# The value columns of the input projection as one token-major product of 512 columns

## The chip, the cores and the metric

The kernel runs on one core of one Trainium2 chip. The metric is the device time of one execution in microseconds (us), lower is better; a kernel's time is the median of its runs. Engines are named as in the profile: PE is TensorE (its matrix products) and PEld its weight loads, DVE is VectorE, ACT is ScalarE, POOL is GpSimd, SP is the queue that issues most transfers from memory (DMA).

## The reference

One layer of a decoder over 1024 tokens of width 1024, all in float32. The part that the change touches is the first projection:

```
h = rms_norm(x, mix_pre_norm)
z = h @ w_in                                   # 1024 x 2816
q_a, k_a, v_a, q_h, f_h, i_h, g_h = split(z)   # 512, 128, 128, 512, 512, 512, 512 columns
attn = sliding_window_sink_attention(q_a, k_a, v_a, sinks)   # the banded part
rec  = hgrn2_group(q_h, f_h, i_h, g_h, ...)    # 4 heads; i_h holds the heads' values
x = x + rms_norm(concat(attn, rec) @ w_out)
```

After it come a cross-attention into 256 memory tokens (4 heads; each head's values times its rows of `ca_wo` is one 256 x 1024 matrix, `VW`), and a gated MLP with a convolution of width 3.

## The kernel before

**Precision.** A float32 product is made of three products of reduced-precision parts: every operand is split into a high part (a cast on ACT) and a rest (a subtraction, on DVE or POOL), and high x high, high x low and low x high are summed in PSUM. `split` (lines 72 to 74) is that pair of instructions; its rows in the profile all carry L73 and L74.

**Layouts.** A product either puts features on partitions (`feat`, `feat_part`: the weight stands, 512 or 256 tokens stream through) or tokens on partitions (`wide_block`: a block of 128 tokens stands, the weight's columns stream). `wide_block` is used where the next step wants tokens on partitions: for the banded attention's values `va` and for the values `vh` of the recurrence's heads 0 to 2 (head 3 goes through `feat` and is transposed). The width 1024 of the contraction is 8 steps `k`, so a block of 128 tokens takes 8 x 3 = 24 products.

**The first token pass** (the loop `for q in range(4)`, lines 275 to 294). Each turn takes two blocks of 128 tokens: their normalised rows are transposed on PE (`turn_block`, L127, 16 transposes), split into `hTh`, `hTl` (L129 on ACT, L132 on DVE), multiplied with the K columns (`feat_part`, L227, 24 products of 256 columns into `pk`), and with a 256-column piece of `w_in` (`wide_block`, L256): 128 columns of `va` and the 128 of head 0. Two turns share one PSUM tile `pv` of four blocks, which ACT then copies out with two instructions of 512 columns (L293, L294). Meanwhile the next two blocks of x are normalised (L89 on ACT, L83 and L84 on POOL, L114 on DVE).

**The four head groups** (`for j in range(4)`, lines 591 to 636). Each makes the banded query `pqa`, and for the recurrence `pg`, `pq`, `pf`, with `feat` (48 products of 512 columns each). At j = 1 a second `wide_block` stage makes heads 1 and 2: 8 blocks, again 256 columns, copied out on L608. Between products, `tick()` lets the two lanes, the banded attention (`swa`) and the recurrence (`hgrn`), issue one step of their work: once every 6 products of 512 columns in `feat`, once every 12 of 256 columns in `wide_block`.

**Weights.** The table `order` lists all weight pieces of these stages in their order of use; `load_next` (lines 161 to 181) issues the loads, and `ahead` (lines 183 to 195) keeps loads and splits a few pieces ahead. Which engine makes the rest of a split is chosen by one expression that uses the piece's index `n` in `order`:

```
t = split_u(t, "w", (P, KD, P) if kind == "cols" else (P, 1024),
            pool if n == 0 or arg[0][0] is a["ca_wo"] and n % 2 else dve)
```

So of the eight pieces of `ca_wo`, two for each head of `VW` (L813), those at odd places of `order` are split on POOL, the others on DVE.

**PSUM.** The pool `pj` holds two tiles of 1024 columns, the pool `sm` four of 512 columns, each taken in turn. Within an engine instructions run in the order that a scheduler gave them when the program was built; `order` rows below show that order.

## Time and profile before

| | before |
|---|---|
| median of three runs | 1417.96 us (1416.31 to 1418.66) |
| the profiled execution | 1420.67 us |
| its span, first to last instruction | 1418.5 us |
| mean granted clock of TensorE | 0.993 |
| PE busy | 1385.2 us, 98% of the span |
| DVE, ACT, POOL busy | 893.1, 649.7, 164.7 us |

A row of the timeline gives the start of an instruction in us from the span's start, how long it took, its engine, line and operation, what it writes and reads with sizes, how many equal ones were merged, and in brackets how long its engine had been idle before it and what ended that. A product's own duration runs over its successor's start, since products are pipelined; what a product occupies PE for is read from start to start.

### The profile page before, as it was taken

What the parts mean: (1) busy time and instruction counts of PE and PEld (TensorE: products, weight loads), DVE (VectorE), ACT (ScalarE), POOL (GpSimd) and SP (SyncE); (2) the same over time, 40 slices, a digit from 0 to 9 for tenths busy, and PEclk for the clock granted to TensorE, in tenths of its full rate; (3) what the DMA queues carried; (4) which work ended last, traced back from release to release, by engine and by line L of the source; (5) the groups of instructions that cost most, each with busy time, mean ns of one, the idle gap of its engine ahead of it and who ended that gap; (6) DMA issues with size and microseconds to landing.
All of it is one profiled execution on the core that took longest, in us unless ns stands there. A gap on an engine that the chain in (4) does not pass through costs nothing.

```text
span 1418.5 us, 21778 instructions
## 1 busy us (share of the span) xinstructions
PE 1385.2 (98%) x8638; PEld 1157.0 (82%) x8638; DVE 893.1 (63%) x1273; ACT 649.7 (46%) x1185; POOL 164.7 (12%) x258
## 2 busy tenths in 40 slices
PE   7999999999999999999999899999999999999997
PEld 6988887877898888887888788888888888788886
DVE  4456617565674553458336998888888887645572
ACT  4463523635464333345334554554554555444440
POOL 3100100101010110002111121111111130000020
PEclk9999999999999999999999999999999999999999
DMA  7231102111843252014222376666655676977651
GB/s 232 53 82 46 46 8 54 31 47 60 209 135 119 90 163 60 7 40 149 89 89 90 86 189 171 177 171 178 170 162 160 168 208 236 328 242 223 223 194 60
DMA packets 157412, 186.04 MB, mean 131 GB/s; under 512 B 17221, under 2 KB 104702, under 8 KB 157310
## 3 DMA queue, kind: packets, MB, share of 16 engines
q1 hardware_dynamic: 145694, 155.81, 35.1%
q0 software_dynamic: 11616, 28.84, 8.6%
q8 instruction: 68, 1.11, 0.3%
q14 instruction: 34, 0.28, 0.1%
HBM read 136.12 MB, written 45.35 MB: 128 GB/s over the span
## 4 chain that ended last, share of the span: by engine, by line
PE 92%; DVE 3%; ACT 2%; DMA 1%; issue 1%; POOL 1%; SPq 1%; DVEq 0%; POOLq 0%; ACTq 0%
PE xz L939 23%; PE dn L1165 14%; PE co L680 6%; PE po L680 6%; PE cq L236 5%; PE y L939 4%; PE pqa L236 3%; PE pm L653 3%; PE pf L236 3%; PE pv L256 3%; PE pq L236 3%; PE pg L236 3%; PE cq L227 2%; PE sc L768 1%; PE po L448 1%; PE lv L463 1%
## 5 line engine op out<-in xcount | busy, mean ns | idle before, releaser
L939 PE MATMUL xz<-th,w 128*128 128x512 f32 x960 | 305.2, 392 | 0.0
L939 PEld LDWEIGHTS xz<-th,w 128*128 128x128 f32 x960 | 180.2, 188 | 44.5 <-DVE ug L1041 4.0
L939 PE MATMUL xz<-tl,w 128*128 128x512 f32 x480 | 187.2, 390 | 0.0
L74 DVE TENSOR_TENSOR dnl<-dn,dnh 128x1024 fp32r<-128x1024 f32 x77 | 90.5, 1219 | 56.0 <-ACT dnh L73 53.6
L1165 PE MATMUL dn<-dnl,dnh 128*128 128x512 f32 x308 | 121.3, 394 | 2.7 <-DVE dnl L74 2.7
L1165 PE MATMUL dn<-dnh,dnl 128*128 128x512 f32 x308 | 121.0, 393 | 0.0
L1165 PE MATMUL dn<-dnh 128*128 128x512 f32 x308 | 120.0, 392 | 0.0
L939 PEld LDWEIGHTS xz<-tl,w 128*128 128x128 f32 x480 | 90.2, 188 | 17.3
L73 ACT CAST dnh<-dn 128x1024 fp32r<-128x1024 f32 x77 | 76.8, 1053 | 48.9 <-PE dn L1165 21.1
L74 DVE TENSOR_TENSOR wl<-w,wh 128x1024 fp32r<-128x1024 f32 x59 | 73.1, 1250 | 29.8 <-ACT wh L73 29.7
L73 ACT CAST wh<-w 128x1024 fp32r<-128x1024 f32 x64 | 66.1, 1052 | 11.7 <-DMA w<-in_ca_wq 4.9
L1165 PEld LDWEIGHTS dn<-dnl,dnh 128*128 128x128 f32 x308 | 58.5, 190 | 15.8 <-DVE dnl L74 3.5
L1165 PEld LDWEIGHTS dn<-dnh,dnl 128*128 128x128 f32 x308 | 58.6, 190 | 12.2
L1165 PEld LDWEIGHTS dn<-dnh 128*128 128x128 f32 x308 | 58.5, 190 | 12.1
L953 DVE SCALAR_TENSOR_TENSOR c<-uv,par,c 128x1023 f32<-128x1023 f32 x22 | 28.2, 1284 | 63.8 <-ACT c L952 63.8
L74 DVE TENSOR_TENSOR w<-w,w 128x512 fp32r<-128x512 f32 x105 | 66.8, 683 | 0.4 <-ACT w L73 0.4
L73 ACT CAST w<-w 128x512 fp32r<-128x512 f32 x105 | 59.6, 618 | 0.0
L939 PE MATMUL y<-th,w 128*128 128x512 f32 x168 | 55.2, 389 | 0.0
L952 ACT ACTIVATE c<-ug,par 128x1024 f32<-128x1024 f32 x22 | 27.4, 1245 | 41.3 <-DVE ug L1041 41.1
L83 POOL TENSOR_SCALAR rstd<-ss 128x1 f32<-128x1 f32 x42 | 14.3, 341 | 230.6 <-ACT y L89 139.0
L680 PE MATMUL po<-wh,mh 128*128 128x512 f32 x128 | 40.0, 393 | 0.0
L680 PE MATMUL co<-VWh,pth 128*128 128x512 f32 x128 | 40.0, 393 | 0.0
(327 smaller groups left out, 3274.9 us busy)
## 6 DMA issues: line engine op xcount, KB each, us to landing
w<-in_ffn_w_up SPq DMA_DIRECT2D x44, 512.0 KB, 5.7
dn<-gd SPq DMA_DIRECT2D x77, 256.0 KB, 4.7
ws<-in_ffn_w_down POOLq DMA_DIRECT2D x66, 256.0 KB, 4.3
gd<-c SPq DMA_DIRECT2D x44, 256.0 KB, 2.3
wsd<-ws POOLq DMA_DIRECT2D x44, 256.0 KB, 2.7
dn<-wsd SPq DMA_DIRECT2D x44, 256.0 KB, 5.0
gd<-gt SPq DMA_DIRECT2D x33, 256.0 KB, 3.3
dn<-in_ffn_w_down SPq DMA_DIRECT2D x33, 256.0 KB, 4.3
```

The costliest lines, as they stand in the source:

```text
L73: act.copy(hi, src)
L74: eng.tensor_tensor(lo, src, hi.bitcast(F32), op=ALU.subtract)
L83: pool.tensor_scalar(r, ss, eps, None, op0=ALU.add)
L227: pe.matmul(ps[:, t0:t0 + n], l[:, k, :], r[:, k % 2, c:c + n], start=(m == 0), stop=(m == 23))
L236: pe.matmul(ps[:, half * 512:(half + 1) * 512], l[:, k, :], hts[half][k // 2][sel][:, k % 2, :], start=(k == 0 and j == 0), stop=(k == KD ...
L256: pe.matmul(ps[:, tb % 4, :], l[:, k % 2, c:c + P], r[:, k % 4, :], start=(m == 0), stop=(m == 23))
L653: pe.matmul(ps[:, i, :], l[:, k, :], r[:, k % 4, :], start=(n == 0), stop=(n == 23))
L680: pe.matmul(ps[:, ch * 512:(ch + 1) * 512], l, r[:, ch * 512:(ch + 1) * 512], start=(k == 0 and j == 0), stop=(k == KD - 1 and j == 2))
L939: pe.matmul(ps, l[k], r[k // 2][:, k % 2, :], start=start and m == 0, stop=stop and m == last, skip_group_check=True)
L952: act.activation(c, u, AF.Identity, scale=conv_w(2, j), bias=conv_b(j))
L953: dve.scalar_tensor_tensor(c[:, 1:], u[:, :T - 1], conv_w(1, j), c[:, 1:], op0=ALU.mult, op1=ALU.add)
L1165: pe.matmul(ps, l[:, 0, c], r[:, 1, :], start=start and k == 0, stop=stop and k == 2, skip_group_check=True)
```

## The change

The 256-column piece becomes one of 512 columns: `va` and heads 0, 1 and 2 together. It is loaded as four tiles of 256 rows of `w_in`, each by two transfers (128 columns and 384 columns), where there were two tiles of 512 rows. All of it is multiplied in the first token pass; the stage at j = 1, its weights and its 16 ticks are gone. A block's result is now one PSUM tile of the pool `sm` (it was a quarter of a `pj` tile), and each block is copied out at once, by four ACT copies of 128 columns.

```
-    order = [cols(w_in, (C_KA, P)), ("wide", [(w_in, C_VA, P), (w_in, C_IH, P)])]
+    order = [cols(w_in, (C_KA, P)), ("wide", [(w_in, C_VA, P), (w_in, C_IH, 3 * P)])]
     for j in range(4):
-        if j == 1:
-            order.append(("wide", [(w_in, C_IH + P, 2 * P)]))
...
-            t = [U("w", (P, 4, 256)) for _ in range(2)]
-            for i in range(2):
+            t = [U("w", (P, 2, 512)) for _ in range(4)]
+            for i in range(4):
                 o = 0
                 for w, c, n in arg:
-                    sp.dma_start(t[i][:, :, o:o + n], w[512 * i:512 * i + 512, c:c + n]
+                    sp.dma_start(t[i][:, :, o:o + n], w[256 * i:256 * i + 256, c:c + n]
                                  .rearrange("(k p) n -> p k n", p=P))
...
-                pe.matmul(ps[:, tb % 4, :], l[:, k % 2, c:c + P], r[:, k % 4, :],
+                pe.matmul(ps, l[:, k % 2, c:c + P], r[:, k % 2, :],
                           start=(m == 0), stop=(m == 23))
                 m += 1
-            if k % 4 == 3:
-                tick()
...
-        if q % 2 == 0:
-            ps_v = PJ("pv", (P, 4, 256))
         for tb in (2 * q, 2 * q + 1):
+            ps_v = SM("pv")
             wide_block(ps_v, first[1], hT, tb)
-        if q % 2 == 1:
-            act.copy(va[:, 2 * q - 2:2 * q + 2, :], ps_v[:, :, :P])
-            act.copy(vh0[:, 2 * q - 2:2 * q + 2, :], ps_v[:, :, P:])
+            for i, t in enumerate([va] + vh[:3]):
+                act.copy(t[:, tb, :], ps_v[:, i * P:(i + 1) * P])
...
-        if j == 1:
-            w = weight()
-            vh[1:3] = [U("vh", (P, NB, P)) for _ in range(2)]
-            for half in range(2):
-                ps = PJ("pv", (P, 4, 256))
-                for b in range(4):
-                    wide_block(ps, w, hT, half * 4 + b)
-                for i in range(2):
-                    act.copy(vh[1 + i][:, half * 4:half * 4 + 4, :], ps[:, :, i * P:(i + 1) * P])
```

Three places of the built order are spoken of below. The first is on PE, at the second turn of the first token pass, from its last transposes on (`tp`; `pk` is the K product, `pv` the value product). Before:

```order
L127 MATMUL tp_313<-ident,x_111 128x128 x4
L256 MATMUL pv_237<-wh_191,hTh_85 128x256
L227 MATMUL pk_127<-hTh_85,wh_147 128x256
L256 MATMUL pv_237<-wl_192,hTh_85 128x256
L256 MATMUL pv_237<-wh_191,hTl_86 128x256
```

and now:

```order
L127 MATMUL tp_338<-ident,x_111 128x128 x4
L225 MATMUL pk_133<-hTh_85,wh_155 128x256
L254 MATMUL pv_385<-wh_199,hTh_85 128x512
L254 MATMUL pv_385<-wl_200,hTh_85 128x512
L254 MATMUL pv_385<-wh_199,hTl_86 128x512
```

The value product, which needs one block's parts, stood ahead of the K product, which needs both blocks'; now the K product stands first.

The second is on ACT at the third turn: the copies out of `pv` and the casts of the transposed blocks. Before:

```order
L293 COPY va_128<-pv_237 128x512
L294 COPY vh_129<-pv_237 128x512
L129 CAST hTh_93<-tp_410 128x2x128
L129 CAST hTh_95<-tp_410 128x2x128
L129 CAST hTh_93<-tp_428 128x2x128
```

and now:

```order
L288 COPY va_134<-pv_414 128x128
L288 COPY vh_135<-pv_414 128x128
L288 COPY vh_136<-pv_414 128x128
L288 COPY vh_137<-pv_414 128x128
L129 CAST hTh_93<-tp_443 128x2x128
L129 CAST hTh_95<-tp_443 128x2x128
L129 CAST hTh_93<-tp_461 128x2x128
```

Two copies of 512 columns ahead of the casts at every second turn have become four of 128 columns at every turn (those of the block that ended last; the other block's stand earlier).

The third is on PE in the cross-attention, at the first head of `VW` (`vw`, made from the `ca_wo` pieces' parts `wh`, `wl`) and the first scores of the last head (`sc`). Before:

```order
L813 MATMUL vw_6394<-wl_6285,cvh_6274 128x512 [waits Pool_49]
L813 MATMUL vw_6448<-wh_6280,cvl_6275 128x512 x2
L768 MATMUL sc_6407<-ckh_6401,cqh_6268 128x256 [waits Activation_49]
L768 MATMUL sc_6464<-ckh_6401,cqh_6268 128x256
L813 MATMUL vw_6448<-wh_6284,cvh_6274 128x512 x2
L768 MATMUL sc_6407<-ckl_6402,cqh_6268 128x256 [waits DVE_49]
```

and now:

```order
L797 MATMUL vw_6232<-wl_6119,cvh_6112 128x512 [waits Pool_49]
L797 MATMUL vw_6286<-wh_6118,cvl_6113 128x512
L752 MATMUL sc_6245<-ckh_6239,cqh_6106 128x256 [waits Activation_49]
L797 MATMUL vw_6286<-wh_6118,cvl_6113 128x512
L752 MATMUL sc_6302<-ckh_6239,cqh_6106 128x256
L797 MATMUL vw_6286<-wh_6122,cvh_6112 128x512 x2
L797 MATMUL vw_6286<-wl_6123,cvh_6112 128x512 x2
L752 MATMUL sc_6245<-ckl_6240,cqh_6106 128x256 [waits DVE_49]
```

One list entry fewer moves every piece of `ca_wo` by one place, so the first piece of each pair is now split on POOL and the second on DVE, the other way round than before; and two products more stand ahead of the score that waits for DVE.

## Rows read from the trace of the kernel before

**Rows 1.** The profile's page: busy time, share of the span, number of instructions.

```profile
PE 1385.2 (98%) x8638; PEld 1157.0 (82%) x8638; DVE 893.1 (63%) x1273; ACT 649.7 (46%) x1185; POOL 164.7 (12%) x258
```

**Rows 2.** PE's longest waits, whole span: for whom, us in total, times, longest.

```profile
PE tp L127 <- DVE x L114: 9.3, 2, 7.9
PE dn L1165 <- DVE dnl L74: 2.7, 1, 2.7
```

**Rows 3.** Line 256: one of three equal forms; ns shortest/median/longest, first and last start.

```profile
L256 PE MATMUL pv<-wh,hTh x128: 277/283/386, 17.9 to 169.1; 128*128 128x256 f32 x128
```

**Rows 4.** Timeline of PE: 37 value products of 256 columns in a row.

```profile
31.20 0.28 PE L256 MATMUL pv<-wh,hTl 128*128 128x256 f32 x1
...
35.52 0.28 PE L256 MATMUL pv<-wh,hTl 128*128 128x256 f32 x1
```

**Rows 5.** Timeline of PE: 17 products of 512 columns in a row.

```profile
186.34 0.62 PE L236 MATMUL pq<-hTh,wh 128*128 128x512 f32 x2
...
189.97 0.39 PE L236 MATMUL pq<-hTh,wl 128*128 128x512 f32 x1
```

**Rows 6.** Timeline of PE: the later turns of the first token pass and its end.

```profile
23.64 1.91 PE L127 MATMUL tp<-ident,x 128*128 128x128 f32 x16
...
27.03 0.38 PE L256 MATMUL pv<-wh,hTl 128*128 128x256 f32 x1 [0.71 <-DVE hTl L132]
...
35.65 1.91 PE L127 MATMUL tp<-ident,x 128*128 128x128 f32 x16
37.31 0.36 PE L256 MATMUL pv<-wh,hTh 128*128 128x256 f32 x1
...
46.42 1.91 PE L127 MATMUL tp<-ident,x 128*128 128x128 f32 x16
...
57.19 0.25 PE L309 MATMUL pst<-ident,pv 97*128 97x97 f32 x1
```

**Rows 7.** Timeline of DVE at the second turn.

```profile
25.36 1.28 DVE L114 SCALAR_TENSOR_TENSOR x<-x,rstd,wmix 128x1024 f32<-128x1024 f32 x1 [0.77 <-POOL rstd L84]
```

**Rows 8.** ACT: timeline at the third turn; then a group (busy us, mean ns).

```profile
35.84 0.59 ACT L293 COPY va<-pv 128x512 f32<-128x512 f32 x1 [9.26 <-PE pv L256]
...
36.80 2.33 ACT L129 CAST hTh<-tp 128x256 fp32r<-128x256 f32 x8
...
L73 ACT CAST mh<-mTa 128x128 fp32r<-128x128 f32 x32 | 7.5, 297 | 1.1 <-PE po L680 1.1
```

**Rows 9.** Timeline of the first 20 us: the value piece's halves and the first value product.

```profile
14.32 1.05 ACT L73 CAST wh<-w 128x1024 fp32r<-128x1024 f32 x1 [0.40 <-DMA w<-in_w_in]
...
16.10 1.04 ACT L73 CAST wh<-w 128x1024 fp32r<-128x1024 f32 x1 [0.73 <-DMA w<-in_w_in]
...
17.18 1.23 DVE L74 TENSOR_TENSOR wl<-w,wh 128x1024 fp32r<-128x1024 f32 x1 [0.55 <-ACT wh L73]
...
17.89 0.28 PE L256 MATMUL pv<-wh,hTh 128*128 128x256 f32 x1
```

**Rows 10.** Timeline of POOL, DVE and PE in the cross-attention, one engine after another.

```profile
638.57 2.67 POOL L74 TENSOR_TENSOR wl<-w,wh 128x1024 fp32r<-128x1024 f32 x1 [9.18 <-ACT wh L73]
...
654.75 2.39 POOL L74 TENSOR_TENSOR wl<-w,wh 128x1024 fp32r<-128x1024 f32 x1 [8.79 <-ACT wh L73]
...
639.04 2.74 DVE L74 TENSOR_TENSOR ckl<-ckT,ckh 128x512 fp32r<-128x512 f32 x1
...
655.25 1.91 DVE L773 TENSOR_SCALAR cmx<-cmx 128x2 f32<-128x2 f32 x1
...
641.83 0.39 PE L768 MATMUL sc<-ckl,cqh 128*128 128x256 f32 x1 [1.45 <-DVE ckl L74]
...
659.03 0.70 PE L813 MATMUL vw<-wh,cvh 128*128 128x512 f32 x2 [2.02 <-DVE cri L780]
```

**Rows 11.** Busy time by stage: PE, PEld, DVE, ACT, POOL, then granted clock, DMA share, GB/s.

```profile
800.00:805.00 5.00, 4.72 (x11) 3.80 (x12) 4.35 (x7) 2.47 (x4) 0.00 (x0) 0.50 0.70 225
...
1220.00:1225.00 5.00, 5.00 (x13) 3.90 (x12) 4.58 (x5) 3.26 (x4) 0.00 (x0) 0.50 1.05 392
```

## The prediction

> **What bounds the kernel now.** The page first: PE is busy for 1385.2 of 1418.5 us [rows 1]. The list of PE's waits comes next: the longest is the start-up, 9.3 us until the first blocks are normalised, the second 2.7 us near the end [rows 2]; the rest is smaller. So what PE has to issue sets the time, and an edit is worth what it takes off PE's issue, plus what it does to the few places where PE waits. Busy shares don't price that, since a product's duration covers its successor's start; from start to start does. 37 value products of 256 columns start from 31.20 to 35.52 us: 4.32 / 36 = 0.120 us each [rows 4]. 17 products of 512 columns start from 186.34 to 189.97 us: 3.63 / 16 = 0.227 us each [rows 5]. Twice 0.120 is 0.240: a product of 512 columns costs 0.013 us less than two of 256.

> **The products.** Three forms of 128 products on line 256 [rows 3] are 384 of 256 columns, 384 x 0.120 = 46.1 us; the change has 8 blocks x 24 = 192 of 512 columns, 192 x 0.227 = 43.6 us. That is **-2.5 us**, all on PE, which has no slack. The column work is the same; only the fixed part of 192 products goes. [...]

> **The turns of the first token pass.** Between two turns PE has 16 transposes (35.65 to 37.31, 1.66 us) and 72 products of 0.120, 8.64 us, together 10.30 us. The three stretches from turn to turn are 12.01, 10.77 and 10.77 us [rows 6], so they lose 1.71, 0.47 and 0.47 us, 2.65 in all. At the second turn PE waits for a DVE subtraction [rows 6] that stood behind the normalisation of a later block, 25.36 to 26.64 us [rows 7]. In the change the two value blocks before that turn take 48 x 0.227 = 10.9 us instead of 5.8, so the turn comes some 5 us later, and that normalisation is done by then: its loss falls to that of the others. On the other side every turn now has four ACT copies ahead of the casts, and the first product behind the transposes is K's. ACT begins 0.19 us after the turn does (35.84 against 35.65), a cast takes 2.33 / 8 = 0.29 us, and the nearest row for a copy of 128 columns is 7.5 / 32 = 0.23 us [rows 8]. The K product waits for the fifth cast at the second and fourth turn, the third cast at the third, by the order on ACT: 0.19 + 0.94 + 1.45 = 2.6 us after the turn's start, or 2.0, where the transposes end at 1.66. Losses: 0.9, 0.35, and 0.7 at the fourth, where the order has one product of the banded query ahead; 1.95 in all. If copies from PSUM are so short that they delay nothing, each turn loses 0.47, 1.4 in all. I take 1.65, the middle: **-1.0 us**; bounds -1.3 and, if nothing is won at the second turn, +0.6.

> PSUM: a value block needs one of four `sm` tiles, shared in turn with the transposes. The first one after a turn gets the tile that the turn's first transposes used, so it waits for two casts and two DVE subtractions, no longer than K waits. I cost it at nothing; if it waited for all eight casts and subtractions (0.19 + 0.94 + 2.33 and 0.4 for the last subtraction, less 1.66, is 2.2 us a turn), the turns would lose 6.6 us, 4.0 more than before, and the whole would come out 1.1 us above it.

> **The start.** The two halves of the value piece (512 KB each) reach ACT at 14.32 and 16.10 us, 1.78 us apart, and the rest of the second is ready at 18.41 [rows 9]. The change has four such tiles; one per 1.78 us puts the fourth at 19.66. Its cast (1.04) and its subtraction (1.23, and 0.04 between) end at 21.97. PE starts the first value block at 17.89 and comes to the fourth tile after 18 of its products, plus one that the order takes from the other block, 17.89 + 19 x 0.227 = 22.2 us. So it is just covered: **0**, with +1 as the bound if a tile takes 0.3 us more. The x blocks behind the piece land some 3.5 us later, but their turns come later by as much or more: nothing.

> **The stage at j = 1.** Its 16 ticks go, but each lane is empty for several ticks of j = 1, so no lane step is left without cover: the recurrence of one head needs 27 ticks and still has 32, the banded attention 19 and has 24. A tick's cover was 12 x 0.120 = 1.44 us and is 6 x 0.227 = 1.36: **0**. The 24 more ACT copies (32 x 0.23 against 8 x 0.59, some 2.7 us) fall on an engine that is busy for 46% [rows 1].

> **The pieces of `ca_wo`.** This part is not meant, but the order shows it: the index moves by one, and POOL splits the other piece of each pair. It matters, because PE's two waits in this stretch, 1.45 us at 641.83 and 2.02 at 659.03, follow DVE instructions that were drawn out while POOL ran a split: 2.74 us for `ckl`, ending 0.54 us after POOL's 638.57 + 2.67, and 1.91 us for a `cmx` of two columns, ending with POOL's 654.75 + 2.39 [rows 10]. Now POOL starts one ACT cast (about 1 us) earlier. At the first place DVE then has its own split ahead of `ckl`, which ends at about 641.9, as late as before, but two more products (0.45 us) stand ahead of the score. At the second POOL's split begins some 1.9 us earlier and meets another small instruction of the same chain; I see no gain there that I can name. I take **-0.4 us**; bounds -3.5 (both waits go) and +2.0 (one more like the longer).

> **The sum** is -2.5 - 1.0 - 0.4 = -3.9 us. The profiled execution took 1420.67, of which 1418.5 is span: the same execution would take 1416.8. The runs' median lies 2.7 us below the profiled one, at 1417.96, and from it I forecast **1414.1 us**.

> **Rivals.**

> (a) The products alone. The copies and K's place at the turns eat what the second turn wins, and the `ca_wo` stretch comes out even: -2.5, 1415.5 us, within 0.2% of before (2.8 us, about what can be told from no change here). For it speaks that the copies stand ahead of the casts at every turn; against it, that the 1.71 us has a cause that a later turn removes. Chance 0.22.

> (b) No gain per product. Rows 5 come from a stage where one weight serves two products in a row; `wide_block` changes both operands each time. If a product of 512 columns then costs 0.240 us, the -2.5 is gone: 1416.6 us. Against it, the loads of weights (PEld) overlap, and as many of them are issued as products [rows 1]. [...] Chance 0.06.

> (c) The `ca_wo` pieces fall badly. POOL's splits hold up DVE where before they met nothing, and PE pays one more wait of about 2 us. Products and turns alone give 1417.96 - 3.5 = 1414.5, so 1416.5 us, within 0.2%. Chance 0.08.

> (d) The `ca_wo` pieces fall well, both waits go: 1414.5 - 3.5 = 1411.0 us. For it speaks only that POOL starts earlier. Chance 0.10.

> (e) Slower: PE waits for POOL itself. The first piece of each head's pair is now split on the slow engine (2.67 and 2.39 us against 1.23 for the same size on DVE) [rows 9, 10], and `VW` wants that piece's rest with its third product. If the pieces are made so late that PE stands through the split, that is some 2.5 us for each of four heads, 10 us: 1417.96 - 3.5 + 10 = 1424.5 us. It decides from (2.8 + 3.5) / 4 = 1.6 us a head on. Against it, POOL's splits end at 641.24 and 657.14, and PE's waits there are put down to DVE, none to POOL [rows 10]. Chance 0.05.

> TensorE's clock moves all of these by a little. [...] I leave it out of the sum and put 2 us on the range's upper end.

> **How the numbers follow.** The forecast has 0.49 and (d) 0.10 on the same side, 0.59 for faster; (a), (b) and (c) 0.36 for the same; (e) 0.05 for slower. The range reaches from (d), 1411.0, less half a microsecond, to (c), 1416.5, plus part of the clock's 2 us: **1410.5 to 1417.8**.

> **What would show it.** 192 products on the value line, 0.227 us from start to start; from turn to turn 15.8 to 16.4 us (1.66 + 24 x 0.120 + 48 x 0.227 = 15.4, plus the loss); no wait of PE at the fourth tile of weights near 22 us; K's first product 2.0 to 2.6 us after a turn's start; in the cross-attention a shorter wait for `ckl`. Wrong if PE waits over 1 us for weights in the first block, if the products start 0.240 us apart, or if the waits of the `ca_wo` stretch add up to more than 5.5 us.

## The result and the profile after

The changed kernel took **1409.91 us** (median of six runs, 1409.67 to 1411.77), the kernel before 1418.49 beside it (1416.31 to 1420.11). The ratio is 0.9937, 95% interval [0.9926, 0.9948]: 8.6 us faster, where 3.9 were forecast. The time lies 0.6 us below the forecast's range. Medians leave out slow runs, one each in three of the later kernels (1531 to 3764 us).

The page of the changed kernel, busy time of the engines (the line that answers to [rows 1]):

```profile
PE 1378.7 (98%) x8446; PEld 1143.1 (81%) x8446; DVE 891.6 (63%) x1273; ACT 654.6 (46%) x1211; POOL 163.2 (12%) x258
```

PE has 192 products less, as built. Where the time went is read from when the same product starts in the two profiled executions (spans 1418.5 and 1408.1 us):

| product | before | after | shift |
|---|---|---|---|
| first of `pm` (memory projection) | 366.46 | 363.35 | -3.1 |
| last of `pm` | 429.64 | 424.71 | -4.9 |
| first of `cq` (cross-attention) | 522.99 | 518.57 | -4.4 |
| first of `co`, behind the `ca_wo` stretch | 668.97 | 662.67 | -6.3 |
| first of `xz` (gated MLP) | 807.77 | 800.72 | -7.1 |
| last of `dn` | 1409.57 | 1399.11 | -10.5 |

Only the first step belongs to the part of the program that was edited. PE's waits in the changed kernel (for whom, us in total, times, longest), some of the list, which answer to [rows 2]:

```profile
PE tp L127 <- DVE x L114: 9.7, 3, 8.0
...
PE dn L1149 <- DVE dnl L74: 2.0, 1, 2.0
...
PE sc L752 <- DVE ckl L74: 0.9, 1, 0.9
PE pk L225 <- ACT hTh L129: 0.8, 2, 0.5
PE vw L797 <- DVE cmx L757: 0.6, 1, 0.6
```

**The edited part.** Timeline of PE: the first value products of the first turn, then the later turns and the end of the first pass (columns as told in front):

```profile
17.82 0.63 PE L254 MATMUL pv<-wh,hTh 128*128 128x512 f32 x2
...
28.74 1.91 PE L127 MATMUL tp<-ident,x 128*128 128x128 f32 x16
31.15 0.39 PE L225 MATMUL pk<-hTh,wh 128*128 128x256 f32 x1 [0.50 <-ACT hTh L129]
...
45.06 1.91 PE L127 MATMUL tp<-ident,x 128*128 128x128 f32 x16
47.00 0.39 PE L225 MATMUL pk<-hTh,wh 128*128 128x256 f32 x1
47.52 0.47 PE L254 MATMUL pv<-wh,hTh 128*128 128x512 f32 x1
...
61.28 1.91 PE L127 MATMUL tp<-ident,x 128*128 128x128 f32 x16
62.94 0.48 PE L234 MATMUL pqa<-hTh,wh 128*128 128x512 f32 x1
63.69 0.38 PE L225 MATMUL pk<-hTh,wh 128*128 128x256 f32 x1 [0.26 <-ACT hTh L129]
...
77.62 0.25 PE L303 MATMUL pst<-ident,pv 97*128 97x97 f32 x1
```

48 products take 28.74 - 17.82 = 10.92 us, 0.227 each, as forecast. The stretches from turn to turn are 16.32, 16.22 and 16.34 us; 1.66 + 24 x 0.120 + 48 x 0.227 = 15.44 of that is work, and in the last 0.23 more for the banded query's product, so the turns lose 0.88, 0.78 and 0.67 us, 2.3 in all, where before lost 2.65 [rows 6]. Rows of ACT and DVE at the second turn (answering to [rows 7, 8]), then of DVE at the third:

```profile
28.94 0.27 ACT L288 COPY va<-pv 128x128 f32<-128x128 f32 x1 [2.38 <-PE pv L254]
29.10 0.61 ACT L288 COPY vh<-pv 128x128 f32<-128x128 f32 x3
29.57 2.36 ACT L129 CAST hTh<-tp 128x256 fp32r<-128x256 f32 x8
...
28.57 1.28 DVE L114 SCALAR_TENSOR_TENSOR x<-x,rstd,wmix 128x1024 f32<-128x1024 f32 x1 [0.77 <-POOL rstd L84]
30.30 2.08 DVE L132 TENSOR_TENSOR hTl<-tp,hTh 128x256 fp32r<-128x256 f32 x6 [0.44 <-ACT hTh L129]
...
46.62 0.76 DVE L132 TENSOR_TENSOR hTl<-tp,hTh 128x256 fp32r<-128x256 f32 x2 [13.59 <-ACT hTh L129]
```

At the second turn the casts begin 0.83 us behind the turn's first transpose, behind the four copies, and the K product waits for ACT; 0.88 us is what the prediction had there (0.9). At the third the K product starts as forecast, 1.94 us after the turn, but the value product behind it starts only 0.52 us later, at 47.52; at the second turn it came 0.22 us behind K. The trace puts the end of its wait down to DVE's subtraction for `hTl`, the second of which ends at 47.38. That product doesn't read `hTl`, so what it waited for is its PSUM tile, which these subtractions still read.

The normalisation at the second turn is not done "by then": it still runs into the turn, as in [rows 7]; no product waits for it any more, since the K product stands first and waits for ACT. At the start the four weight tiles came one per 1.47 us (casts at 13.92, 15.35, 16.84, 18.32), faster than forecast, and PE waits for none.

**The `ca_wo` stretch.** POOL, DVE and PE there, which answer to [rows 10]:

```profile
633.21 2.41 POOL L74 TENSOR_TENSOR wl<-w,wh 128x1024 fp32r<-128x1024 f32 x1 [10.16 <-ACT wh L73]
637.05 2.52 POOL L74 TENSOR_TENSOR wl<-w,wh 128x1024 fp32r<-128x1024 f32 x1 [1.43 <-ACT wh L73]
...
634.12 2.59 DVE L74 TENSOR_TENSOR wl<-w,wh 128x1024 fp32r<-128x1024 f32 x1 [0.67 <-ACT wh L73]
636.63 0.68 DVE L74 TENSOR_TENSOR ckl<-ckT,ckh 128x512 fp32r<-128x512 f32 x1
638.36 1.76 DVE L74 TENSOR_TENSOR cvl<-cv,cvh 128x512 fp32r<-128x512 f32 x1
...
646.85 2.53 POOL L74 TENSOR_TENSOR wl<-w,wh 128x1024 fp32r<-128x1024 f32 x1 [7.27 <-ACT wh L73]
647.75 1.65 DVE L757 TENSOR_SCALAR cmx<-cmx 128x2 f32<-128x2 f32 x1
...
652.98 0.16 DVE L757 TENSOR_SCALAR cmx<-cmx 128x2 f32<-128x2 f32 x1
...
637.36 0.39 PE L752 MATMUL sc<-ckl,cqh 128*128 128x256 f32 x1 [0.94 <-DVE ckl L74]
653.21 0.70 PE L797 MATMUL vw<-wh,cvh 128*128 128x512 f32 x2 [0.62 <-DVE cmx L757]
```

DVE is still held up while POOL runs a split (2.59 us for a `wl` that takes 1.22 alone), but it is now the `wl` ahead and the `cvl` behind (1.76 us, 0.68 alone) that pay; `ckl` takes 0.68 instead of 2.74. At the second place POOL's split again draws out a small `cmx`, to 1.65 us, but one that ends 3.8 us ahead of the waiting product at 653.21; the `cmx` just ahead of that product takes 0.16 us. The two waits go from 1.45 + 2.02 to 0.94 + 0.62 us: 1.9 us, where 0.4 were forecast. Why a split on POOL draws out a DVE instruction, `ckl` to 2.74 us and `cmx` to 1.91 and 1.65, is not shown by any run here.

**The memory projection.** Here the kernel before has an idle stretch that the prediction passed over. PE's timeline of before, then of after, at the same burst of 32-column products:

```profile
374.60 0.68 PE L463 MATMUL lv<-qP,kS 128*32 128x32 f32 x55
376.90 0.28 PE L463 MATMUL lv<-qP,kS 128*32 128x32 f32 x9 [1.62 <-issue]
```

```profile
371.49 0.76 PE L457 MATMUL lv<-qP,kS 128*32 128x32 f32 x64
```

64 products that are done in 0.76 us broke off after 55, and PE stood for 1.62 us with nothing that released it ("issue").

**The clock.** Granted clock by stretches, in before, then in after (us busy of PE, PEld, DVE, ACT, POOL, then the clock, DMA share, GB/s), answering to [rows 11]:

```profile
798.50:805.50 7.00, 5.22 (x13) 4.17 (x14) 6.31 (x9) 3.97 (x6) 0.27 (x1) 0.51 0.61 197
1219.00:1225.00 6.00, 5.95 (x14) 4.74 (x15) 5.58 (x6) 4.20 (x4) 0.00 (x0) 0.50 1.05 393
```

```profile
794.80:798.20 3.40, 3.40 (x10) 2.66 (x9) 3.40 (x6) 1.37 (x2) 0.00 (x0) 0.51 0.55 160
1211.50:1216.50 5.00, 5.00 (x22) 4.15 (x23) 4.62 (x4) 4.00 (x4) 0.00 (x0) 1.00 1.05 396
```

Behind the same waits of PE (2.4 us for `w` near 800 us in both, 2.7 and 2.0 us for `dnl` near 1216 and 1209), TensorE ran at a granted clock of 0.50 to 0.51 for half as long at the first place and not at all at the second. These two make up the last 4 us of the table, as the second execution of the kernel before shows, whose first fall was as short and which had no second: from `co` to `xz` 138.09 us, from `xz` to the last `dn` 598.43, as in the changed kernel (138.05 and 598.39), where the first execution took 138.80 and 601.80.

### The profile page after: what moved, and what is told of

Read it like the earlier page. It is cut to its first block, busy times and chain, and to the rows that moved or that the text cites. A ratio compares the mean times of both kernels' runs of the same rounds, so it can differ in the third digit from the quotient of the medians.

```text
span 1408.1 us, 21436 instructions
## 1 busy us (share of the span) xinstructions
PE 1378.7 (98%) x8446; PEld 1143.1 (81%) x8446; DVE 891.6 (63%) x1273; ACT 654.6 (46%) x1211; POOL 163.2 (12%) x258
## 4 chain that ended last, share of the span: by engine, by line
PE 92%; DVE 3%; ACT 2%; DMA 1%; issue 0%; POOL 0%; SPq 0%; DVEq 0%; POOLq 0%; ACTq 0%
PE xz L923 23%; PE dn L1149 14%; PE co L664 6%; PE po L664 5%; PE cq L234 5%; PE y L923 4%; PE pqa L234 3%; PE pm L637 3%; PE pv L254 3%; PE pf L234 3%; PE pq L234 3%; PE pg L234 3%; PE cq L225 2%; PE sc L752 1%; PE po L442 1%; PE lv L457 1%
## 5 line engine op out<-in xcount | busy, mean ns | idle before, releaser
L74 DVE TENSOR_TENSOR dnl<-dn,dnh 128x1024 fp32r<-128x1024 f32 x77 | 90.5, 1219 | 53.4 <-ACT dnh L73 47.8
L74 DVE TENSOR_TENSOR wl<-w,wh 128x1024 fp32r<-128x1024 f32 x59 | 72.7, 1242 | 15.4 <-ACT wh L73 15.2
```

The lines of the kernel that those rows point to most:

```text
L74: eng.tensor_tensor(lo, src, hi.bitcast(F32), op=ALU.subtract)
```

## The experiments

Theory: the edit itself gives the products' 2.5 us and little more; the rest are three side effects, the parity of the `ca_wo` pieces (1.9), the idle stretch (1.6), and the clock. The rivals are told with each.

**The kernel before again, and the parity alone in either kernel.** The first is unchanged; the others change one expression, in the kernel before to the new parity, in the changed kernel back to the old.

```
...
-                            pool if n == 0 or arg[0][0] is a["ca_wo"] and n % 2 else dve)
+                            pool if n == 0 or arg[0][0] is a["ca_wo"] and n % 2 == 0 else dve)
...
```

> The kernel before, unchanged, profiled a second time. Three things in its first trace go beyond the sum on record: an idle stretch of 1.62 us without a releaser in a run of 32-column products (line 463, near 376 us), and two stretches of 6.8 us at half the granted clock, from 798.55 and from 1219 us. Theory A (fixed by the program, by the place of each instruction or by the length of the wait ahead): all three come again, at the same places, within 0.3 us. Theory B (chance of one execution): at least one of the three is missing or moved, and the span differs from 1418.5 us by what it cost, 1.6 us for the idle stretch and some 2.5 us for a clock stretch. Time by both: 1416 to 1420.5 us.

> The kernel before with nothing changed but the parity: the first piece of each ca_wo pair is split on POOL. Theory A (the change of parity shortens PE's waits for ckl and cmx by itself, as in the changed kernel, 1.45 and 2.02 to 0.94 and 0.62 us): the first co product comes 1.9 us earlier than before against the first vw, and the median is 1.5 to 2.2 us below before's. Rival: the shorter waits come from everything arriving 4.4 us earlier, with loads and other engines at other phases; then the waits stay at 3.0 us or more and the time within 0.5 us of before's. The idle stretch in line 463 stays under both, if it is the program's.

> The changed kernel with the old parity: the second piece of each ca_wo pair on POOL. Theory A (parity): the two waits come back, 3.0 to 3.6 us together, and the time is 1.5 to 2.2 us above the changed kernel's 1409.9, near 1411.8. Rival (phase): the time stays at 1409.5 to 1410.4. Up to the first vw (about 620 us) its trace is the changed kernel's: first mem_proj product at 363.3, last at 424.7, no idle stretch in line 463.

The kernel before: 1418.91 us. The idle stretch came again at the same product, 1.47 us long, but the falls of the clock were others. Of its profile:

```profile
376.47 0.28 PE L463 MATMUL lv<-qP,kS 128*32 128x32 f32 x9 [1.47 <-issue]
```

```profile
658.80:662.00 3.20, 3.20 (x9) 2.52 (x8) 2.04 (x3) 0.33 (x1) 0.00 (x0) 0.50 0.03 6
802.00:805.50 3.50, 3.50 (x10) 2.72 (x9) 3.46 (x6) 1.52 (x2) 0.00 (x0) 0.51 0.58 174
1218.00:1223.00 5.00, 4.18 (x18) 3.49 (x19) 4.49 (x5) 3.16 (x3) 0.00 (x0) 1.00 1.05 399
```

So the idle stretch belongs to the program (theory A for it) and the falls to the execution (theory B): the wait at 1216 us was followed by a fall in one execution and not in the other, and the one for `vw` near 658 the other way round. With the new parity the kernel before took 1416.77 us, 1.6 less, and the `ca_wo` stretch is 1.9 us shorter, waits 0.96 and 0.55. With the old parity the changed kernel took 1414.27, 4.4 above its 1409.91, and its waits are 1.49 and 1.85. Theory A's 1.9 leaves 2.5 us; the mean clock of these runs, 0.9948 against 0.9972, is about that much (see below, 0.001 for some 1 us). Timeline of PE with the old parity in the changed kernel:

```profile
636.98 0.39 PE L752 MATMUL sc<-ckl,cqh 128*128 128x256 f32 x1 [1.49 <-DVE ckl L74]
654.00 0.70 PE L797 MATMUL vw<-wh,cvh 128*128 128x512 f32 x2 [1.85 <-DVE cri L764]
```

Both waits follow the parity, in either kernel; that all comes earlier in the changed kernel is not what shortened them.

**Each value product as two.** The changed kernel, but:

```
...
-                pe.matmul(ps, l[:, k % 2, c:c + P], r[:, k % 2, :],
-                          start=(m == 0), stop=(m == 23))
+                for o in (0, 256):
+                    pe.matmul(ps[:, o:o + 256], l[:, k % 2, c:c + P], r[:, k % 2, o:o + 256],
+                              start=(m == 0 and o == 0), stop=(m == 23), skip_group_check=True)
...
```

> The changed kernel with every value product of 512 columns as two of 256 columns, the block's two products for one contraction step next to each other; loads, copies, pools and the place of everything else as in the changed kernel. [...] Idle stretch in line 463: PE has again 192 more instructions ahead of it, as in the kernel before. If the stretch depends on how many instructions PE has behind it, it comes back (1.6 us, in all 4.1 above the changed kernel, 1414.0); if it doesn't, 1412.4.

1414.12 us, where 1414.0 was expected with the idle stretch and 1412.4 without; both have the 2.5 us of the prediction's products in them. The first turn's value products and the idle stretch:

```profile
17.16 0.40 PE L255 MATMUL pv<-wh,hTh 128*128 128x256 f32 x2
...
28.69 1.91 PE L127 MATMUL tp<-ident,x 128*128 128x128 f32 x16
...
375.17 0.33 PE L458 MATMUL lv<-qP,kS 128*32 128x32 f32 x15 [1.27 <-issue]
```

96 products take 11.53 us, 0.120 each, against 10.92 for the 48: 0.61 a turn, 2.5 in four. The first `pm` came at 365.12, only 1.8 later than in the changed kernel, because this execution had gained 0.66 us before (its value products begin at 17.16 instead of 17.82): its first K products went over from 0.21 us apart to 0.12 at 15.4 us, those of the changed kernel at 16.6. The products' term stands. And the idle stretch is back, although the stage at j = 1 is not.

**What the idle stretch is.** Row 3 of the page (queue, packets, MB, share) has an instruction queue; before and after:

```profile
q8 instruction: 68, 1.11, 0.3%
```

```profile
q8 instruction: 66, 1.08, 0.3%
```

```
...
-    ps_k = PJ("pk")
+    ps_k = PJ("pk"); [pe.transpose(ps_k[:8, :8], ident[:8, :8], ident[:8, :8]) for _ in range(64)]
...
```

> The kernel before with 64 tiny transposes (8 x 8) ahead of the first real one, while PE stands idle anyway; the rest of every engine's order is unchanged. PE's stream moves by 128 instructions (64 loads, 64 products), half of a 16 KB packet of the instruction queue if an instruction takes 64 bytes. Theory (the idle stretch of 1.0 to 1.6 us in the 32-column products near 376 us is PE running out of fetched instructions, and comes from where the packets' bounds fall in the burst): it is gone, as in the changed kernel, whose stream is shorter by 384 instructions, one and a half packets; the first to the last mem_proj product take 61.4 us instead of 63.0 to 63.2, and the time is 1.5 us below before's. Rival (the change of data or order at j = 1 removed it): it stays, and the time is before's. [...]

> The changed kernel with the same 64 tiny transposes ahead. Theory: its stream now stands at the kernel before's place within the packets (384 - 128 = 256 instructions, one whole packet, less), so the idle stretch of 1.0 to 1.6 us comes back in the 32-column products near 371 us and the time is 1.5 us above the changed kernel's. Rival: no idle stretch, the changed kernel's time.

The kernel before with them: 1417.81 us, 1.0 below the kernel before of the same runs (ratio 0.9992, interval [0.9980, 1.0004], not clear of noise); the burst runs through, and `pm` takes 61.4 us from its first to its last product (63.2 without). The changed kernel with them: 1413.16 us, 3.2 above the changed kernel of the same runs (1409.99); the stretch is there. Their bursts, in that order:

```profile
374.47 0.76 PE L463 MATMUL lv<-qP,kS 128*32 128x32 f32 x64
```

```profile
371.15 0.63 PE L457 MATMUL lv<-qP,kS 128*32 128x32 f32 x49
372.81 0.33 PE L457 MATMUL lv<-qP,kS 128*32 128x32 f32 x15 [1.02 <-issue]
```

The traces are as the theory has it: 128 instructions of no work take the stretch away from one kernel and give it to the other. The times, 1.0 and 3.2 us where 1.5 was forecast for either, are not; of the 3.2 some 1 us goes with the clock (0.9958 against 0.9968) and some 1 us isn't accounted for. In six profiles of the kernel before and its variants with its stream the stretch was 0.6 to 1.6 us long.

Two counts in the traces go further. Over loads, products and PE's semaphore instructions, the product ahead of which PE stopped comes 192 or 193 instructions after a multiple of 256 in all ten traces that have such a stop, of either kernel, though it is the 19th of its burst in one and the 56th in another. And in all ten PE goes on 1.3 to 1.6 us after a packet of the instruction queue has ended (in the kernel before the packet ran from 374.10 to 375.27, and the product starts at 376.90). From this the author takes it that PE was waiting for that packet; the list of waits names no releaser. In the changed kernel, shorter by 384 instructions, one packet and a half, that place falls into the next burst, at 374.28, and the packet had ended at 371.90.

**No split on POOL, and the copies on DVE.** In the changed kernel `pool if n == 0 else dve` keeps all `ca_wo` pieces on DVE; beside it the changed kernel again.

> The changed kernel with every ca_wo piece split on DVE, none on POOL. Theory (the waits for ckl and cmx come from DVE instructions drawn out while POOL runs a split): ckl takes 0.7 us or less, cmx 0.3 us or less, both waits together fall from 1.56 us to under 1.0 us, and the time is 0.5 to 1.0 us below the changed kernel's. Rival (DVE has 1.25 us more of work per piece ahead of ckl and cmx, and they end as late): the waits stay at 1.5 us or grow, time the same or up to 1 us above.

> The changed kernel once more, on the chip of these runs. Its six runs had a mean granted clock of 0.997 where 41 runs of the kernel before had 0.995 in the mean, and a run's time goes down by some 1 us for each 0.001. Theory A (the change removed a wait of 2 us in the cross-attention, so a fall behind it is rarer, and shortened nothing else: most of the clock's difference was chance): mean clock 0.996, median 1410.5 to 1411.5. Theory B (the change gives a better clock for good): 0.997 and 1409.5 to 1410.2.

The changed kernel again took 1409.99 us (mean clock 0.9968), as theory B of its expectation has it. Without POOL both waits are gone (no such row among PE's waits), `ckl` takes 0.69 us, and from the first `vw` to the first `co` product it is 1.8 us less than in the changed kernel (29.86 for 31.70); but the time was 1409.79, 0.2 below and not the 0.5 to 1.0 forecast, with a mean clock of 0.9958. DVE without splits on POOL:

```profile
634.91 0.69 DVE L74 TENSOR_TENSOR ckl<-ckT,ckh 128x512 fp32r<-128x512 f32 x1
```

The same again in more runs, with the copies out of PSUM moved to DVE (`dve.tensor_copy` for `act.copy` on line 288) alone and together:

> The kernel with all ca_wo splits on DVE once more, in more runs. Its first profile has neither the wait for ckl nor that for cmx, 2.1 us less from the first vw to the first co product than the changed kernel. Theory: the median is 1.5 to 3 us below the changed kernel's in the same runs (2.1 us of waits, and a clock that falls no more often). Rival: the earlier work meets a longer wait at the start of the dn stage, and half or more of it is given back; then 0 to 1 us below.

> The changed kernel beside the others of these runs. Earlier medians 1409.91 (6 runs, mean clock 0.9972) and 1409.99 (4 runs, 0.9968). If the better clock is the change's, 1409.5 to 1410.5 with a mean clock of 0.9965 or more; if it was chance, 1410.5 to 1411.8 with 0.996 or less.

> The changed kernel with its value copies out of PSUM on DVE and not on ACT; PE has as many instructions as before, DVE 32 more. In the changed kernel the stretches from turn to turn are 16.22 to 16.34 us, 0.78 to 0.90 more than the products and transposes take, and the K product starts 1.94 to 2.41 us after a turn's start. Theory (the four ACT copies ahead of the casts cost the casts 0.6 us): the K product starts 0.4 to 0.6 us sooner at the turns where it waited, and the stretches are 15.8 to 15.9 us, in all some 1.2 us less. Rival (DVE's copies hold up the subtractions for hTl, and PE waits for these or for PSUM instead): the stretches stay at 16.2 us or become longer.

> Both edits: ca_wo splits on DVE alone, and the value copies on DVE. They touch different stretches, so their gains should add up: 2.1 and, if the copies' theory holds, 1.2 us below the changed kernel, 1406.5 to 1407.5 us; if the copies bring nothing, 1407.5 to 1408.5.

The changed kernel took 1411.54 (clock 0.9958 this time, the value that its expectation gives to chance), without POOL 1409.82, 1.7 less, with the copies on DVE 1410.86, 0.7 less, with both **1407.62** (0.9926 of before, [0.9909, 0.9943]), the fastest kernel found, 3.9 us below the changed one of the same runs. Of the 3.9, some 1 us goes with the clock (0.9968 in the runs with both); the traces have 1.8 and 0.8. The copies bring less than expected: stretches of 16.06, 16.00 and 16.07 us instead of 16.22 to 16.34, 0.8 us in all. Timeline of PE with the copies on DVE:

```profile
29.36 1.91 PE L127 MATMUL tp<-ident,x 128*128 128x128 f32 x16
31.52 0.39 PE L225 MATMUL pk<-hTh,wh 128*128 128x256 f32 x1 [0.26 <-ACT hTh L129]
```

The K product starts 2.16 us after the turn, not 2.41: the casts themselves take most of it. With both edits a stop of 0.4 us ("issue") appeared in a burst of 32-column products, though PE's stream is as long as in the changed kernel. It is at the same place in 256, in the burst that the changed kernel runs through, but that burst begins at 373.34 instead of 374.28, and the packet ended at 372.84 instead of 371.90; so the place alone does not make a stop: the burst begins 0.50 us after the packet's end here and 2.38 us after it there.

**The clock.** Over all runs whose clock is known, the mean granted clock of the kernel before was 0.9949 (116 runs), the changed kernel's 0.9966 (15), and within each kernel a run is some 1 us longer for 0.001 less. On the one chip where both were taken side by side it is less, 0.9952 (29) and 0.9962 (9). At equal clock the two differ by less than 8.6: at 0.996 1417.4 (16 runs) and 1411.3 (5), at 0.997 1416.0 (10) and 1409.9 (5), some 6 us; at 0.995 and 0.998, with two and three runs of the changed kernel, 7.3 and 6.4. Was the wait for `cmx`, which the parity shortens, one of the places where the clock falls?

> The kernel before with every ca_wo split on DVE: both waits of the ca_wo stretch should go (1.45 and 2.02 us), with nothing else of the change made. Theory A (the wait there was one of the places where the clock fell): the mean granted clock rises from 0.9951 to 0.996 or more, and the median is 4.5 us or more below before's, 3.5 to 4.0 us of waits and about 1 us of clock. Theory B (the clock's difference was chance): 0.9946 to 0.9956, and 3.5 to 4.0 us below.

> The changed kernel with the old parity once more. Nine runs before had a mean clock of 0.9948, median 1414.3. Theory A: again 0.9955 or less and 1413.5 to 1414.8, 3.5 us or more above the changed kernel, of which 1.9 to 2.1 are the two waits. Theory B: 0.996 or more, and 1412 to 1413.

> The kernel before with the parity of the changed one, once more. Ten runs before had a mean clock of 0.9956 and a mean 2.2 us below before's. Theory A: 0.9956 to 0.9966, 2.2 to 3.3 us below before's. Theory B: 0.995, 1.9 us below.

The kernel before without splits on POOL: 1414.82 us, 3.9 below before, mean clock 0.9952, which is theory B. The changed kernel with the old parity: 1414.10 and 0.9948, which is theory A. The kernel before with the new parity: 1416.28 and 0.9955, between. The waits alone don't give the clock. The twenty traces say what they can: near 800 us, behind a wait of 2.4 us, the clock fell in all; behind the wait for `vw` in two of the six where that wait was 1.85 to 2.02 us, and in none of the others, where it was 0.65 or less; behind the wait for `dn` in six, with waits of 2.23 to 2.82 us, and not in fourteen, with waits of 1.90 to 2.82. The last test moves PE's later waits in time, with 7 more products of 512 columns (`hTh` by `wh` into `pst`, overwritten) ahead of line 303, or 309 in the kernel before:

> The changed kernel with 7 more products of 512 columns near 77 us, whose result is overwritten: 7 x 0.227 = 1.6 us later from there on, every engine's order unchanged. If the clock depends on when the later waits come, its mean moves away from 0.9966, to 0.995 or less, and the time is 2.5 to 3.5 us above the changed kernel's 1410.2; if it belongs to the kernel, or is chance, 0.996 to 0.997 and 1.6 us above, 1411.8.

> The kernel before with the same 7 products near 57 us, 1.6 us later from there on. If the clock depends on when the waits come, its mean rises from 0.9950, to 0.9958 or more, and the time is less than 1 us above before's; if it belongs to the kernel, or is chance, 0.9947 to 0.9954 and 1.6 us above.

The changed kernel with them: 1413.34 us, mean clock 0.9957, so 3.2 us more than the 1410.2 of all its runs where the work is 1.6. Its profile:

```profile
793.80:800.60 6.80, 6.23 (x15) 4.88 (x16) 6.15 (x8) 3.59 (x5) 1.28 (x2) 0.50 0.71 226
1213.60:1217.00 3.40, 3.34 (x8) 2.66 (x9) 3.03 (x4) 2.52 (x3) 0.00 (x0) 0.50 1.05 396
```

The kernel before with them: 1420.41 us and 0.9949, where the kernel before of the same runs had 1419.31 and 0.9945: 1.1 more. Neither settles it. In the changed kernel the time is as the place in time would have it, but the clock isn't down to 0.995, and with nothing moved it had been 0.9958 in five runs, at 1411.54; against these the 7 products cost 1.8. In the kernel before the clock didn't rise to 0.9958. A third kernel, with 15 products in the changed one, had 0.9968 and 1413.37 us, but a stop of 1.66 us in the burst at 377 came with it, so it says little of the clock. What gives the changed kernel the better clock, or whether it is chance, stays open.

## Why the prediction was wrong

By its own steps, with what each measured:

- **The products**, -2.5: right. 0.120 and 0.227 us from start to start, 0.61 a turn, which is 13 ns for each of 48 products less.
- **The turns**, -1.0: over-sized. They lose 2.3 us where 1.65 were forecast, so the gain was 0.3. The step that failed is the PSUM tile, of which the prediction said that a value product waits for it "no longer than K waits", and which it costed at nothing: at the third turn the K product did start 1.94 us after it, as forecast, but the value product behind it waited for the subtractions, and the loss was 0.78 for 0.35. The other 0.3 is the middle that was taken between 1.95 and 1.4; 1.95 was nearer. On the other side 0.3 us more, by difference, was gained between the first pass and `pm`, where the stage at j = 1 was costed at nothing; together the edited part gave 3.1 where 3.5 were forecast.
- **The start**, 0: right; the tiles came faster than the estimate from the larger ones.
- **The `ca_wo` pieces**, -0.4: mis-sized, measured -1.9 in the profile; from the first `vw` to the first `co` product the parity alone is worth 1.9 us in the kernel before and 1.7 in the changed one. The first wait came as reasoned, 0.5 us shorter for 0.45. The step that failed is the second: "I see no gain there that I can name", where 1.4 us was gained. POOL's split did meet another small instruction of the chain, as the prediction says, but one with 3.8 us to spare ahead of the product that waited. The mechanism (POOL's split holds up DVE: `ckl` 2.74 us beside one, 0.69 with none on POOL) and the bounds (-3.5 to +2.0) were right. Rival (d), at 1411.0, is both waits gone; 1.56 of 3.47 us stayed, and they go only without splits on POOL.
- **Left out: the idle stretch.** The list of PE's waits that [rows 2] comes from has 1.6 us with "issue" as releaser. The prediction summed it under "the rest is smaller". It has no releaser to reason about; the experiments tie it to PE's own instruction stream (128 instructions ahead took it from the kernel before and gave the changed one 1.02 us), which the change moved by 384 instructions. Worth 0.6 to 1.6 us.
- **The clock**, left out of the sum with 2 us on the upper end only. No run shows these 2 us as a bound: [rows 11] have 11 and 13 products in 5 us at a granted clock of 0.50, where 5 / 0.227 = 22 fit, so 2.0 to 2.5 us go in those 5 us alone, and the whole second fall of the kernel before cost 3.4 us. The two profiles of the kernel before and the three of the changed kernel show that the falls differ between executions of one program; but the mean over 15 and 116 runs differs by 0.0017, some 1.5 to 2 us, and that lay on the other side.

The sum with the measured terms: 2.5 + 0.3 + 0.3 + 1.9 + about 1.2 is 6.2 us, as the runs of equal clock have it (6 to 7); with the clock, some 8 of the 8.6. That the clock's part belongs to the change is not shown. The sign and the products were foreseen; more than half the gain came from places that the edit doesn't touch.

Rivals: (a) is refuted, since the stretch of the `ca_wo` pieces did not come out even, and the edit's own part was 3.1. (b) is refuted by 0.227, (c) by the two waits, which became shorter, and (e) since PE's waits in the changed kernel have none for POOL.

## What to carry over

Read each of the engine's waits, those without a releaser too, and ask of each what sets its place: a change that alters the number of instructions, or an index that a rule takes the parity of, moves things far from the edit. Take a wait that two engines make together by its row (DVE 2.74 us against 0.68 alone) and remove the meeting rather than shift it: all splits on DVE were worth 3.9 us in the kernel before (0.2 and 1.7 in two comparisons with the changed one, whose waits were shorter). Where a kernel's time varies with the granted clock, compare runs of equal clock before adding up a mechanism.

## What was not expected of the hardware

- PE stood with no releaser in a burst of 64 loads and 64 products of 32 columns that otherwise takes 0.76 us: for 0.4 to 1.7 us, in all ten traces 192 or 193 instructions after a multiple of 256 and until 1.3 to 1.6 us after the end of a 16 KB packet of the instruction queue. In the kernel before the burst ran through with 128 instructions put ahead. That PE had run out of instructions is the author's reading of these counts.
- In these streams two products of 256 columns took 13 ns more than one of 512, in a block whose both operands change each time too: 0.120 and 0.227 us on the value line itself.
- The granted clock fell to 0.50 behind waits of PE of 1.9 to 2.8 us in some executions and not in others of the same program, and the length of a fall differs (3.4 and 7 us near 800 us). A run with 0.001 less in the mean was some 1 us longer.
